# Split weights of w_in kept in DRAM and loaded back, in one inference step of a hybrid backbone

## The chip, the core and the metric

The kernel runs on one core of one Trainium2 chip, as one program that is launched once. The metric is the time on the device in microseconds (us), the median of several runs. The five engines have their own instruction queues, which run in order: PE (TensorE) multiplies matrices, DVE (VectorE) and POOL (GpSimd) do elementwise work, ACT (ScalarE) does activations and copies, and SP (SyncE) issues nearly all transfers between DRAM and the on-chip memory. An instruction that waits on a semaphore holds what stands behind it in its queue.

## The reference

One layer of a backbone is computed for two groups of tokens with the same weights: 256 context tokens and 2,048 latent tokens, each with 1,024 channels, in float32.

```python
h = rms_norm(x, norm1_g) * (1 + sc1) + sh1        # adaLN: sh1, sc1 ... from silu(cond) @ ada_w
z = h @ w_in                                      # 1024 -> 10 column blocks of 256
a_val, a_gate, g_u, g_v, h_q, h_i, h_g, h_ff, h_fb, s5_u = split(z, 10)
o_conv = conformer_conv(a_val, a_gate, ...)       # GLU, depthwise convolution of width 31, LayerNorm, swish
o_gm = chunk_gmlp(g_u, g_v, ...)                  # spatial gating in chunks of 128 positions
o_hg = hgrn_mixer(h_q, h_i, h_g, h_ff, h_fb, ...) # bidirectional gated recurrence, 4 heads of 64
o_s5 = s5_mixer(s5_u, ...)                        # bidirectional diagonal state space, GELU, GLU
x = x + g1 * (concat(o_conv, o_gm, o_hg, o_s5) @ w_out)
x = x + g2 * (relu(h2 @ mlp_w1) ** 2 @ mlp_w2)    # h2: RMSNorm of x, modulated; 1024 -> 4096 -> 1024
y = rms_norm(x, final_norm_g)
```

The scans of the latents start from given states; the final states of the context scans are outputs too.

## The kernel before, in words

**Three products for one.** Large products are made from two parts of each operand: a high part in the type float32r, which is the value rounded by a copy, and a low part, which is the value less its high part. PE adds three products, high by high, low by high and high by low (`gemm_cm`, lines 167 to 176, for channel-major results; `gemm_tm`, lines 558 to 563, for token-major ones). Weights come in units of 128 x 1,024 elements, 0.5 MB each; with a full token block, `gemm_cm` runs 24 matmuls of 512 columns on one unit.

**A unit's way.** `load_unit` (line 162) takes one of three raw tiles `wraw`, has SP load the unit, and calls `split_unit` (line 150). There ACT copies it to a tile `whi` (line 152) and the low part goes to a tile `wlo`, by two halves on POOL (line 157) or by one instruction on DVE (line 159). The argument `pool_only` gives all to POOL (the first pass); otherwise a running count gives every second (second pass) or third unit (third pass) to POOL and the others to DVE. There are four `whi` and four `wlo` tiles, each free again when PE has used it.

**Token blocks and passes.** The tokens are cut into five blocks: the context (256 tokens) and four of 512 latents. The first pass takes blocks 1, 2, 3, 4, 0. For each, `pass1_t` makes values of the recurrence and inputs of the state space, token by token tile, from four units at once; `pass1_g` makes queries and forget gates of two heads at a time, with three units each; `hgrn_local` works inside chunks, in seven levels that pass from PE to DVE, POOL and ACT and back. For the first block `first_block` does most of this with loads of its own, interleaved with the adaLN products, and asks for one unit in `first_out` only. The second pass (`pass2`) takes blocks 0, 1, 2, 3, 4 and asks for ten units for each: four for the convolution's input, two token-major ones at once for the gMLP, two for its other operand, two for the recurrence's output gate. Each block thus loads and splits the units of `w_in` again. Beside the second pass run the state space's scans (`s5_ctx`, `s5_lat`), the first convolutions (`conv`) and the remaining adaLN products (`ada_late`). The third pass (`mix_out`, `mlp_up`, `mlp_down`, `final`) takes `w_out` and the MLP's weights, 368 units of a total of 470.

**What sets the order.** The program is written as generators that are stepped in turn (from line 1297 on). A planner then fixes each engine's order by simulated times and dependencies and places the semaphores; tiles of one tag share a fixed number of buffers, and who writes a buffer next waits until all uses of the tile before it are over. A load thus waits in SP's queue for its buffer, and every transfer behind it in SP's order waits with it.

Of the kernel before, what the change touches and what calls it, by code (L numbers as in the profile page):

```python
# [40 lines left out]
# token blocks: (first token, tokens, conditioning row)  # L41
# [8 lines left out]
# blocks in the order of the first pass; the second starts with the last of them  # L50
# [3 lines left out]
class Carve:  # L54
    """Tiles cut from one, by tag, as from a pool."""
# [19 lines left out]
def trunk_kernel(ctx, tc, I, O):  # L75
# [3 lines left out]
    # ------------------------------------------------------------------ pools  # L79
# [8 lines left out]
    def nm(s):  # L88
        uid[0] += 1
        return f"{s}_{uid[0]}"  # L90
# [19 lines left out]
    # -------------------------------------------------------------- constants  # L110
# [27 lines left out]
    def lower_bounds():  # L138
        """Of the forget gates: cumsum of a softmax over the layers less its first term."""
        V.tensor_tensor(lb, lbl, lbl, ALU.subtract)  # L140
        A.activation(lb, lb, AF.Exp)
        V.reciprocal(lbt, lb)
        V.tensor_tensor(lb, lb, lbt, ALU.mult)
        V.tensor_tensor(lb, lb, lb, ALU.subtract)
        V.tensor_scalar(omlb, lb, -1.0, 1.0, ALU.mult, ALU.add)

    # --------------------------------------------------- weights: load, split
    nlo = [0]

    def split_unit(raw, pool_only, w=1024, every=3):  # L150
        hi = wts.tile([128, 1024], F32R, tag="whi", name=nm("whi"), bufs=4)
        A.activation(hi[:, :w], raw[:, :w], AF.Copy)  # L152
        lo = wts.tile([128, 1024], F32R, tag="wlo", name=nm("wlo"), bufs=4)
# [12 lines left out]

    def gemm_cm(ps, n, unit, hs, ts=None):
        """ps[128 cols, n tokens] = unit[8 k x 128 cols]^T @ hs, of the tokens ts."""
# [9 lines left out]
    # ------------------------------------------------------ adaLN: chunks 0, 1  # L178
# [6 lines left out]
    # ------------------------------------------------------------ DRAM scratch  # L185
# [16 lines left out]
    # ----------------------------------------------------------------- helpers  # L202
    def xblock(pool, b, bufs=1, w=None, halves=1, engs=None, pos=False):
        """x of a block, channel-major, with the position signal on latents."""
# [20 lines left out]
    def rms_rstd(pool, x8, n, eng=None, ps=None, cols=False):  # L225
        """1 / sqrt(mean over channels of x^2 + eps), on every partition."""
# [14 lines left out]
    def rstd_sums(sq, n, ps, heads=1):  # L241
        """Column i * heads + h of ps: sums of sq over a head's channels, for the tokens of tile i."""
# [4 lines left out]
    def rstd_rows(n, scale, ps, heads=1, in_place=False, sums=None):  # L247
        """1 / sqrt(sums * scale + eps), token by token, then spread over the partitions of a head."""
# [30 lines left out]
    def modulate1(pool, hpool, x8, n, rstd, gain, shift, k, w=512, t=None):  # L279
        """hi and lo parts of a channel tile of x * rstd * gain + shift."""  # L280
# [11 lines left out]
    # --------------------------------------------------- S5: tables of a layer  # L292
# [9 lines left out]
    def cmul(eng, o, a, b, tmp):  # L302
        """o = a * b, complex; o may not be a or b."""
# [7 lines left out]
    def s5_small(sp):  # L311
# [10 lines left out]
        # dt = exp(log_dt): Taylor at a 16th of it, then four squarings  # L322
# [8 lines left out]
        # e1 = exp(a_re dt) - 1 by doubling, mag = exp(a_re dt)  # L331
# [42 lines left out]
        # (a_bar - 1) / A  # L374
# [24 lines left out]
        # modulus of a_bar ** 8  # L399
# [3 lines left out]
        # phases e^{i theta n} of the chunk-to-chunk frame, n = 1..16 and n = 0, 16, .., 240  # L403
        V.memset(pc[0][:, :, 0:1], 1.0)
        V.memset(pc[1][:, :, 0:1], 0.0)
        for t_, off, one in ((pb, 0, (u8r.unsqueeze(2), u8i.unsqueeze(2))),
# [3 lines left out]
            m = 1  # L410
# [9 lines left out]
    def s5_tables(sp, scr, small):  # L420
# [12 lines left out]
        # B's for the kernels: a column of 16 each for forward, backward and their sum  # L433
# [3 lines left out]
        # a_bar^m of a quarter's groups, twice over  # L437
# [5 lines left out]
        # the phases of the context, n = 1..32  # L443
# [9 lines left out]
        def cm(o, a, br, bi, g_, n):  # L453
            """o = a * b; o and a [128, (re, im), g_, n], b's parts [128, g_]."""
# [6 lines left out]
        for q in range(4):  # L461
            gs = slice(4 * q, 4 * q + 4)
            # t[:, re or im, 0..3, d] = a_bar^d b_bar and t[:, re or im, 4..7, d] = a_bar^d C^T of the groups
# [12 lines left out]
            # what a chunk's inputs leave in its state, [(dir, p), (s, c)] -> [(s, c), (dir, p)]  # L476
# [10 lines left out]
            # what the state that enters a chunk adds to its outputs  # L487
# [8 lines left out]
            # within a chunk: both directions' kernels, the skip on the diagonal  # L496
# [19 lines left out]
    def s5_kernels():  # L516
        """The kernels within a chunk, spread over its pairs of positions."""
# [4 lines left out]
    # ---------------------------------------------------- adaLN: chunks 2 to 5  # L522
# [14 lines left out]
    # --------------------------------------- first pass: HGRN2 inside of chunks  # L537
# [20 lines left out]
    def gemm_tm(ps, w, xs, wh, wl, first, last):  # L558
        """ps[128 tokens, columns] (+)= x^T @ w, of a channel tile."""
# [32 lines left out]
    def pass1_t(b, hs, p1):  # L592
        """Values of HGRN2 and inputs of S5, token-major."""
        us = [load_unit(I["w_p1t"][i]) for i in range(4)]
# [9 lines left out]
    def pass1_g(b, pair, hs, p1):  # L604
        """Queries and forget gates of two heads; a head's directions share the partitions
        (forward below, backward above), the heads follow each other along the tokens."""
        n = BLOCKS[b][1]
        ps = pg()
        gemm_cm(ps, n, load_unit(I["w_p1c"][3 * pair]), hs)
        qn = q_out(b, ps, p1)  # L610
        f = f_tile(p1)
        for hh in range(2):
            ps = pg()
            gemm_cm(ps, n, load_unit(I["w_p1c"][3 * pair + 1 + hh]), hs)
            f_out(b, 2 * pair + hh, ps, f)
# [8 lines left out]
    def ada_unit(pt, aws, c32, rpool, blocks):  # L624
        """Two blocks of 128 of the adaLN outputs. aws: the weights, four channel tiles each; a tile's
        products go to the partitions of its own, and sel adds them up and turns them."""
# [968 lines left out]
```

## Time and profile before

| what | us |
|---|---|
| median of 3 timed runs | 2892.96 |
| lowest and highest | 2891.01 and 2896.34 |
| span of the profiled execution, first to last instruction | 2886.1 |
| PE busy in that span | 2727.9 (95%) |
| DVE busy | 1975.1 (68%) |
| ACT busy | 1192.9 (41%) |
| POOL busy | 1078.2 (37%) |

The profile is of one execution; its own time is its span, and what the timed runs count beside it lies around the span. The transfers moved 407.43 MB, a mean of 141 GB/s. A busy share is an average over stages with different limits, and matmuls are pipelined, so that PE's busy time is not PE at its peak.

### The profile page before, as it was taken

The numbers are of one execution on the slowest core, as the hardware profiler recorded it, in microseconds if no ns is written. First come the engines' busy times: TensorE is split into PE (matmuls) and PEld (weight loads), VectorE is DVE, ScalarE is ACT, GpSimd is POOL, SyncE is SP. The second block draws the span as 40 slices with busy tenths as digits, with TensorE's granted clock in tenths as the row PEclk, the third lists the DMA queues.
The fourth block names the chain that finished last, engine by engine and source line by source line (L and its number), as shares of the span: only waits on it lengthen the run. The fifth ranks groups of instructions, "written<-read, shape, count | busy, mean of one in ns | idle before, by whom it ended". The sixth has DMA issues, their size and how long they took to land.

```text
span 2886.1 us, 38466 instructions
## 1 busy us (share of the span) xinstructions
PE 2727.9 (95%) x14376; PEld 2260.3 (78%) x14376; DVE 1975.1 (68%) x2786; ACT 1192.9 (41%) x1784; POOL 1078.2 (37%) x915
## 2 busy tenths in 40 slices
PE   6897988899988979999999999999999999999998
PEld 4676878887766769987788888788887888888888
DVE  9889888887799987659973474953384334553336
ACT  4755655553533445443322342332343233433323
POOL 4467757533554534343221232221342111511113
PEclk8999999999999999999999999999999999999999
DMA  8563433357766656634333333333343333233233
GB/s 282 178 187 131 135 118 100 107 167 246 231 188 216 215 197 209 185 124 124 110 102 95 124 123 124 104 101 96 124 149 103 95 98 124 89 131 95 89 101 125
DMA packets 183402, 407.43 MB, mean 141 GB/s; under 512 B 39856, under 2 KB 69680, under 8 KB 182192
## 3 DMA queue, kind: packets, MB, share of 16 engines
q1 hardware_dynamic: 181056, 403.79, 43.4%
q8 instruction: 114, 1.87, 0.3%
q10 hardware_dynamic: 2160, 1.18, 0.1%
q14 instruction: 72, 0.59, 0.1%
HBM read 344.68 MB, written 56.56 MB: 139 GB/s over the span
## 4 chain that ended last, share of the span: by engine, by line
PE 65%; DVE 19%; DMA 2%; issue 2%; POOL 1%; ACT 1%; SPq 0%; DVEq 0%; ACTq 0%; POOLq 0%
PE pg L176 20%; PE pg L175 20%; PE pg L174 20%; DVE x L1166 4%; PE psc L769 2%; DVE wlo L159 1%; DVE m L979 1%; DMA x<-uD 1%; DVE q L775 1%; DVE gg L987 1%; DVE hh L996 1%; DVE pa L271 1%; DVE q L774 1%; DVE kt L773 1%; DVE at L790 1%
## 5 line engine op out<-in xcount | busy, mean ns | idle before, releaser
L174 PE MATMUL pg<-hi,whi 128*128 128x512 f32 (+1 forms) x3488 | 1285.8, 371 | 19.5 <-ACT f L589 5.0
L176 PE MATMUL pg<-hi,wlo 128*128 128x512 f32 (+1 forms) x3488 | 1290.2, 371 | 5.4 <-DVE wlo L159 5.4
L175 PE MATMUL pg<-lo,whi 128*128 128x512 f32 (+1 forms) x3488 | 1288.5, 370 | 3.5 <-DVE lo L286 2.1
L157 POOL TENSOR_TENSOR wlo<-wraw,whi 128x512 fp32r<-128x512 f32 (+1 forms) x404 | 592.1, 1488 | 1281.6 <-ACT whi L152 1198.5
L152 ACT ACTIVATE whi<-wraw 128x1024 fp32r<-128x1024 f32 (+1 forms) x470 | 494.1, 1054 | 873.2 <-PE pg L175 769.9
L174 PEld LDWEIGHTS pg<-hi,whi 128*128 128x128 f32 x3488 | 659.2, 189 | 145.5 <-issue 6.2
L175 PEld LDWEIGHTS pg<-lo,whi 128*128 128x128 f32 x3488 | 659.9, 189 | 129.1 <-issue 7.3
L176 PEld LDWEIGHTS pg<-hi,wlo 128*128 128x128 f32 x3488 | 660.2, 189 | 123.6 <-issue 6.2
L159 DVE TENSOR_TENSOR wlo<-wraw,whi 128x1024 fp32r<-128x1024 f32 x268 | 343.8, 1284 | 198.3 <-ACT whi L152 184.6
L1239 DVE SCALAR_TENSOR_TENSOR x<-pg,adaT,x 128x512 f32<-128x512 f32 (+1 forms) x168 | 111.8, 667 | 283.6 <-PE pg L176 283.1
L1166 DVE SCALAR_TENSOR_TENSOR x<-x,cvw 128x512 f32<-128x512 f32 (+1 forms) x300 | 222.9, 790 | 0.3
L1224 DVE TENSOR_TENSOR t<-t 128x512 f32<-128x512 f32 (+1 forms) x160 | 136.9, 856 | 84.5 <-ACT t L1223 84.5
L1226 ACT ACTIVATE hi<-t 128x512 fp32r<-128x512 f32 (+1 forms) x160 | 94.1, 589 | 240.2 <-DVE t L1224 240.2
L1227 DVE TENSOR_TENSOR lo<-t,hi 128x512 fp32r<-128x512 f32 (+1 forms) x160 | 123.6, 776 | 68.2 <-ACT hi L1226 67.2
L234 POOL TENSOR_TENSOR sq<-sq,sq 128x512 f32<-128x512 f32 (+1 forms) x56 | 87.9, 1570 | 107.8 <-ACT sq L230 107.8
L773 POOL TENSOR_TENSOR kt<-kt,tnx 64x256 f32<-64x256 f32 (+1 forms) x120 | 95.1, 805 | 56.4 <-issue 36.8
L1207 DVE SCALAR_TENSOR_TENSOR x<-pg,adaT,x 128x512 f32<-128x512 f32 (+1 forms) x40 | 27.7, 696 | 112.1 <-PE pg L176 112.1
L230 ACT ACTIVATE sq<-x 128x512 f32<-128x512 f32 (+1 forms) x120 | 66.4, 557 | 81.9 <-DVE sq L234 23.2
L1223 ACT ACTIVATE t<-pg 128x512 f32<-128x512 f32 (+1 forms) x160 | 85.9, 538 | 1.8 <-PE pg L176 1.8
L769 PE MATMUL psc<-qz,kt 128*128 128x128 f32 x432 | 61.0, 299 | 22.8 <-DVE at L790 15.2
L769 PE MATMUL psc<-qzr,kt 128*128 128x128 f32 x576 | 77.1, 286 | 4.3 <-DVE kt L773 3.4
L286 DVE SCALAR_TENSOR_TENSOR lo<-hm,adaT,hi 128x512 fp32r<-128x512 f32 (+1 forms) x72 | 75.8, 1076 | 6.1 <-ACT hi L285 5.2
(372 smaller groups left out, 2982.5 us busy)
## 6 DMA issues: line engine op xcount, KB each, us to landing
wraw<-in_mlp_w_dram SPq DMA_DIRECT2D x328, 512.0 KB, 3.5
wraw<-in_w_p2c_dram SPq DMA_DIRECT2D x40, 512.0 KB, 3.9
wraw<-in_w_out_dram SPq DMA_DIRECT2D x40, 512.0 KB, 3.6
awt<-in_ada_w_dram SPq DMA_DIRECT2D x32, 512.0 KB, 5.6
wraw<-in_w_p1c_dram SPq DMA_DIRECT2D x28, 512.0 KB, 3.6
x<-in_xT_dram SPq DMA_DIRECT2D x16, 512.0 KB, 6.4
aw<-in_ada_w_dram SPq DMA_DIRECT2D x8, 1024.0 KB, 7.3
hD<-hi SPq DMA_DIRECT2D x32, 256.0 KB, 3.3
```

The lines of the kernel that those rows point to most:

```text
L152: A.activation(hi[:, :w], raw[:, :w], AF.Copy)
L157: G.tensor_tensor(lo[:, h_], raw[:, h_], f32(hi[:, h_]), ALU.subtract)
L159: V.tensor_tensor(lo[:, :w], raw[:, :w], f32(hi[:, :w]), ALU.subtract)
L174: PE.matmul(ps[:, :n], wh, xh[:, ts], start=k == 0, stop=False)
L175: PE.matmul(ps[:, :n], wh, xl[:, ts], start=False, stop=False)
L176: PE.matmul(ps[:, :n], wl, xh[:, ts], start=False, stop=k == 7)
L769: PE.matmul(sc[:, s_], kt[:, s_], z[:, s_], start=True, stop=True)
L773: eng.tensor_tensor(kv, kv, tb(lo_, hi_, 1 - half)[:, hs_, :], ALU.mult)
L1166: V.scalar_tensor_tensor(acc[i][:, :n], u2[:, i, k:k + n], cvw[:, i, k:k + 1], acc[i][:, :n], ALU.mult, ALU.add)
L1224: V.tensor_tensor(r, r, r, ALU.mult)
L1227: V.tensor_tensor(lo, r, f32(hi), ALU.subtract)
L1239: V.scalar_tensor_tensor(x8[:, o, ts], ps[:, :n], adaT[:, 40 + o, c:c + 1], x8[:, o, ts], ALU.mult, ALU.add)
```

## The change

The two tiles `whi` and `wlo` of a unit become one tile `whl` that holds both parts, again with four buffers. A new function `kept_unit` takes the place of `load_unit` where weights of `w_in` are asked for. The first time a unit is asked for it is loaded and split as before, and both parts, 1 MB, are stored to a DRAM tile of its own. Each later time both parts are loaded from there by one transfer into the `whl` tile; no raw tile is used and nothing is split. The running count then does not move. `first_block` keeps its own loads, and the weights of `w_out` and the MLP go through `load_unit` as before. The diff also drops comments, which are left out here.

```diff
-    def split_unit(raw, pool_only, w=1024, every=3):
-        hi = wts.tile([128, 1024], F32R, tag="whi", name=nm("whi"), bufs=4)
+    def wtile():
+        return wts.tile([128, 2, 1024], F32R, tag="whl", name=nm("whl"), bufs=4)
+
+    def split_unit(raw, pool_only, w=1024, every=3, t=None):
+        t = t or wtile()
+        hi, lo = t[:, 0, :], t[:, 1, :]
         A.activation(hi[:, :w], raw[:, :w], AF.Copy)
-        lo = wts.tile([128, 1024], F32R, tag="wlo", name=nm("wlo"), bufs=4)
         nlo[0] += 1
...
+    kept = {}
+
+    def kept_unit(name, i, pool_only=True, every=3, keep=True):
+        t = wtile()
+        if (name, i) in kept:
+            SP.dma_start(f32(t), f32(kept[name, i]))
+            return t[:, 0, :], t[:, 1, :]
+        raw = wts.tile([128, 1024], F32, tag="wraw", name=nm("wraw"), bufs=3)
+        SP.dma_start(raw, I[name][i])
+        split_unit(raw, pool_only, every=every, t=t)
+        kept[name, i] = dt_(f"{name}_hl{i}", [128, 2, 1024], F32R)
+        SP.dma_start(f32(kept[name, i]), f32(t))
+        return t[:, 0, :], t[:, 1, :]
...
-        us = [load_unit(I["w_p1t"][i]) for i in range(4)]
+        us = [kept_unit("w_p1t", i) for i in range(4)]
...
-        gemm_cm(ps, n, load_unit(I["w_p1c"][3 * pair]), hs)
+        gemm_cm(ps, n, kept_unit("w_p1c", 3 * pair), hs)
...
-            gemm_cm(ps, n, load_unit(I["w_p1c"][3 * pair + 1 + hh]), hs)
+            gemm_cm(ps, n, kept_unit("w_p1c", 3 * pair + 1 + hh), hs)
...
-        gemm_cm(ps, n, load_unit(I["w_p1c"][2]), hs)
+        gemm_cm(ps, n, kept_unit("w_p1c", 2), hs)
...
-            gemm_cm(pgate, n, load_unit(I["w_p2c"][2 + i], False, 2), hs)
+            gemm_cm(pgate, n, kept_unit("w_p2c", 2 + i, False, 2), hs)
...
-            gemm_cm(pv, n, load_unit(I["w_p2c"][i], False, 2), hs)
+            gemm_cm(pv, n, kept_unit("w_p2c", i, False, 2), hs)
...
-        us = [load_unit(I["w_p2t"][i], False, 2) for i in range(2)]
+        us = [kept_unit("w_p2t", i, False, 2) for i in range(2)]
...
-            gemm_cm(pu, n, load_unit(I["w_p2c"][4 + pair], False, 2), hs)
+            gemm_cm(pu, n, kept_unit("w_p2c", 4 + pair, False, 2), hs)
...
-            gemm_cm(pz, n, load_unit(I["w_p2c"][6 + pair], False, 2), hs)
+            gemm_cm(pz, n, kept_unit("w_p2c", 6 + pair, False, 2), hs)
```

## Rows read from the trace of the kernel before

**Rows 1.** The profile's page, part 2: busy tenths in 40 slices of the span.
```profile
PE   6897988899988979999999999999999999999998
DVE  9889888887799987659973474953384334553336
```

**Rows 2.** Windows: length, busy us of PE, PEld, DVE, ACT, POOL; clock, DMA, GB/s.
```profile
170.00:490.00 320.00, 284.44 (x1665) 244.44 (x1664) 279.57 (x375) 184.30 (x284) 220.01 (x203) 0.95 0.38 122
570.00:930.00 360.00, 325.39 (x2045) 262.84 (x2044) 316.78 (x550) 151.01 (x275) 170.03 (x191) 0.95 0.65 213
650.00:700.00 50.00, 48.59 (x254) 38.99 (x253) 40.66 (x79) 13.98 (x22) 10.28 (x10) 0.90 0.86 301
850.00:900.00 50.00, 43.50 (x239) 32.32 (x232) 49.68 (x76) 18.38 (x27) 23.71 (x25) 0.90 0.73 245
1450.00:1500.00 50.00, 49.80 (x216) 40.04 (x215) 44.45 (x55) 12.28 (x14) 12.45 (x7) 1.00 0.33 106
```

**Rows 3.** Chain of waits by line, 250:600 us, then 720:1060 us.
```profile
by line: PE psc L769 13.8%; PE pg L174 8.5%; PE pg L175 8.2%; PE pg L176 8.2%; DVE q L775 6.3%; DVE q L774 4.8%; DVE kt L773 4.7%; issue 4.6%; DVE at L790 4.5%; PE psc L811 3.0%; DVE Sl L838 3.0%; POOL x L222 2.9%; PE psc L737 2.1%; PE psc 
by line: DVE x L1166 11.2%; DVE m L979 9.7%; issue 6.5%; DVE gg L987 5.8%; DVE hh L996 5.7%; DVE wlo L159 4.8%; DVE pa L271 4.6%; DVE hh L995 4.4%; PE pg L174 4.4%; PE pg L175 4.3%; PE pg L176 4.1%; PE pg L1080 1.7%; DMA x<-mixD 1.7%; PE pg
```

**Rows 4.** Windows of L157 alone: length, POOL's busy us (instructions).
```profile
170.00:490.00 320.00, 94.74 (x63) 0.95 0.38 122
300.00:350.00 50.00, 28.59 (x18) 1.00 0.37 112
350.00:400.00 50.00, 2.52 (x2) 0.93 0.45 156
570.00:930.00 360.00, 55.58 (x40) 0.95 0.65 213
```

**Rows 5.** Window of L159 alone: length, DVE's busy us (instructions).
```profile
570.00:930.00 360.00, 27.27 (x20) 0.95 0.65 213
```

**Rows 6.** The page, part 5: line L152 in the whole run.
```profile
L152 ACT ACTIVATE whi<-wraw 128x1024 fp32r<-128x1024 f32 (+1 forms) x470 | 494.1, 1054 | 873.2 <-PE pg L175 769.9
```

**Rows 7.** Groups by form, DVE, 170:490 us: busy us, mean ns.
```profile
L775 DVE TENSOR_TENSOR q<-q,tnx 64x512 f32<-64x512 f32 x38 | 41.7, 1100 | 1.1
L773 DVE TENSOR_TENSOR kt<-kt,tnx 64x256 f32<-64x256 f32 x70 | 41.3, 605 | 12.1 <-PE psc L769 11.8
L774 DVE TENSOR_TENSOR q<-q,tnx 64x512 f32<-64x512 f32 x38 | 37.4, 987 | 3.1 <-ACT qz L762 2.0 <-DVE tnx L782 0.5
```

**Rows 8.** Single lines: L775 in 300:350, then L775 and L773 in 350:400.
```profile
L775 DVE TENSOR_TENSOR q<-q,tnx x6: 691/1666/1679, 303.7 to 345.1; 64x512 f32<-64x512 f32 x6
L775 DVE TENSOR_TENSOR q<-q,tnx x6: 687/689/690, 362.7 to 398.1; 64x512 f32<-64x512 f32 x6
L773 DVE TENSOR_TENSOR kt<-kt,tnx x14: 397/413/970, 352.4 to 399.9; 64x256 f32<-64x256 f32 x14
```

**Rows 9.** Groups by form, DVE, 570:930 us.
```profile
L1166 DVE SCALAR_TENSOR_TENSOR x<-x,cvw 128x512 f32<-128x512 f32 x58 | 50.5, 893 | 0.3
```

**Rows 10.** Single line: L1166 in 1350:1500 us.
```profile
L1166 DVE SCALAR_TENSOR_TENSOR x<-x,cvw x97: 732/740/1790, 1350.2 to 1486.5; 128x512 f32<-128x512 f32 x97
```

**Rows 11.** Waits of SP's DMA queue, 0:1100 us: total us, times, longest us.
```profile
SPq L164 <- POOL wlo L157: 136.0, 52, 5.8
SPq L164 <- DVE wlo L159: 81.3, 19, 9.8
```

**Rows 12.** Waits of ACT, 600:1060 us.
```profile
ACT whi L152 <- PE pg L175: 45.7, 15, 17.8
```

**Rows 13.** DMA issues of the whole run: KB each, median us to landing.
```profile
wraw<-in_w_p1t_dram SPq DMA_DIRECT2D x16, 512.0 KB, 3.5
wraw<-in_w_p2t_dram SPq DMA_DIRECT2D x10, 512.0 KB, 5.3
x<-in_xT_dram SPq DMA_DIRECT2D x1, 1024.0 KB, 5.1
aw<-in_ada_w_dram SPq DMA_DIRECT2D x8, 1024.0 KB, 7.3
```

## The prediction

> **What bounds the kernel now.** I read the picture of forty slices first. TensorE (PE) shows nearly full slices from about 1,150 us to the end; ahead of that its digits move between 6 and 9, and there VectorE (DVE) carries the 8s and 9s [rows 1]. So only the first 1,150 us have time to give back, and the changed lines lie inside them. The two stretches where weights of `w_in` would be reloaded are 170:490 us (rest of the first pass) and 570:930 us (second pass behind its first block). In the first PE is busy 284 of 320 us and DVE 280; in the second 325 and 317 of 360 [rows 2]. Looked at closer, from 850 to 900 us DVE is full (49.7 of 50) while PE is not (43.5) [rows 2].
>
> PE's busy time also flatters it, since matmuls overlap. A saturated stretch, 1450:1500 us, fits 216 matmuls of 512 columns, one per 0.23 us, so a unit of 24 takes 5.6 us; in 850:900 us, where none has more columns and many have fewer, only 239 stand in the same 50 us [rows 2]. The page "Perfetto Trace Analysis" of the Trainium skill (Identifying the Most-Contended Engine) says to judge TensorE by weight loads, not by matmul busy time; by it PE in 850:900 us, at 32.3 us of loads against 40.0 in the saturated stretch, would have about a fifth of its time to spare, not the 6.5 us of the busy column. This trace agrees.
>
> The chain of waits says the same: in 720:1060 us it runs mainly through DVE lines, L159, the low parts of weights, among them with 4.8% of 340 us, 16 us. In 250:600 us it alternates between PE (L769 and the products) and DVE (L773 to L775, L790) [rows 3]. The first pass is a ping-pong of two engines; the second is bound by DVE.
>
> **The change, part by part.** Counting calls: the first pass asks for 44 units (16 token-major and 28 column ones), the second for 50. Of these 94, 20 are first uses, which are split as before and then stored; 74 become reloads: 34 in the first pass, 40 in the second. A reload is one transfer of 1 MB instead of 0.5 MB, with no ACT copy, no subtraction and no raw tile.
>
> *Removed from ACT and POOL.* The 74 copies at 1.05 us are 78 us of ACT [rows 6]. The stretch 170:490 us holds 63 POOL halves (94.7 of POOL's 220 us); 570:930 us holds 40 halves (55.6 of 170 us) and 20 low parts on DVE (27.3 us) [rows 2, 4, 5]. Nearly all of these belong to reloads after the change. Neither ACT nor POOL is full, so their 78 and 150 us are not a gain by themselves; they matter through what they hold up.
>
> *First pass: DVE's stalls beside POOL.* DVE's operations get long when POOL runs splits. L775 takes 1,666 ns (median) in 300:350 us and 689 ns in 350:400 us [rows 8]; the first of these holds 18 halves, the second 2, while POOL's other work goes on [rows 4]. Against the medians of 350:400 us, the means over 170:490 us cost L775 38 x (1,100 - 689) = 15.6 us, L774, of the same shape, 38 x (987 - 689) = 11.3 us and L773 70 x (605 - 413) = 13.4 us, 40 us together [rows 7, 8]. Shared by POOL's time the splits own 94.7 / 220 of it, 17 us; at the other end all 40. The 300:350 row is the nearest, so I take 28 us. "SBUF — State Buffer" of the Trainium skill (Who interferes with whom) calls this an exclusive lock that the later instruction waits out whole; by that, each of the 63 halves could cost up to its own 1.5 us, 95 us in all. The rows hold no more than the 40 us in these lines, so the sum stays with them. What reaches the end: DVE is busy 87% of this stretch, but PE is nearly as full, and the splits run just where the products run on PE. I pass on a bit under half: **13 us** (ends 0 and 40).
>
> *Second pass: direct DVE work and stalls.* The 20 low parts, 27.3 us, leave the engine that bounds [rows 5]. To this come stalls beside 40 fewer POOL halves: the convolution alone is 58 x (893 - 740) = 9 us longer than its median in 1350:1500 us [rows 9, 10]. POOL's splits are a third of POOL's time there, but other DVE lines gain too; I take 8 us (ends 3 and 15). Of 35 us some falls where DVE is not full, before 750 us: passing three quarters on gives **26 us** (ends 10 and 42).
>
> *Blocked queues.* ACT's copy waits for PE to free a weight buffer, 45.7 us in 15 waits between 600 and 1060 us, one of them 17.8 us [rows 12]; behind it in ACT's queue stand the S5 scan's evacuations, which DVE and PE want. With a reload that wait moves to SP. Ends 0 and 20; most of these waits lie under a busy DVE, so **5 us**.
>
> *Added: later weights.* Today three raw tiles are fetched ahead of the four split buffers. A reload writes into a split buffer itself, so it starts only when PE is done with the unit four before it, and its wait stands at the head of SP's queue; behind it wait the loads of h, the stores of results and the S5 tables, and PE, DVE and ACT behind those. In a run of column units three buffers hold 3 x 5.6 = 16.7 us of products, and a 1 MB load lands in 5.1 us (the one of x) to 7.3 us (adaLN's weights, on busy queues) [rows 2, 13], so it is hidden. It is not where all buffers empty together: the first-pass step that uses four units at once (three times with reloads), and more weakly the two-unit gMLP step of the second pass (four times). There the next unit was split in about 1.05 + 1.5 us (a copy and a POOL half) from a raw tile already there and now needs 5.1 to 7.3 us: 2.6 to 4.8 us more, at 3 to 7 places: **8 us** lost (ends 0 and 34).
>
> *Added: traffic.* 39 MB more loads and 21 MB of stores on SP's queue. In 570:930 us 40 x 0.52 MB add 58 GB/s to 213, and the share of the DMA engines goes from 0.65 to about 0.83; 650:700 us shows that 0.86 at 301 GB/s can be had [rows 2]. The stores follow the first splits, ten ahead of 170 us and ten between the two stretches; PE holds the buffer for products meanwhile anyway. I cost them at nothing; if a store holds SP or a buffer, up to 20 x 1 us. The third pass is untouched, except that the one-in-three turn of POOL and DVE shifts by one unit (74 fewer counts), worth nothing either way.
>
> Sum: 13 + 26 + 5 - 8 = 36 us. The profiled span is 2,886.1 us, so 2,850 after; the median of the timed runs lies 6.9 us above that span (2,892.96), which I keep: **2,857 us**.
>
> **The rivals.** *More of it comes through.* If the ping-pong of the first pass is really DVE's, and blocked queues cost what they show, the relief is 40 + 35 + 20 us with no loss: 2,893 - 95 = 2,798 us at the far end, 2,815 as a middle. For: DVE's 87 to 99% busy columns; against: PE is as full in the first pass.
>
> *It goes nowhere.* Both stretches could be bound by the round trips between PE, ACT and DVE, so that shorter DVE work only lengthens its waits: gain under 6 us, 2,890 us. For: the chain in 250:600 us is mixed [rows 3]; against: 20 instructions leave a stretch that is 99% busy.
>
> *Slower: SP runs dry of buffers.* A reload waits for PE and holds all of SP's queue, with three raw tiles of lead gone. SP already waits 136 us for POOL's and 81 us for DVE's low parts ahead of weight loads, up to 9.8 us at a time [rows 11]. If at the seven places where buffers empty together the next unit comes 10 us late (such a wait, rather than a landing alone), that is 70 us against 44 us of gain: 2,893 + 26 = 2,919 us. It decides from 44 / 7 = 6.3 us a place. For: loads in busy stretches land later, 5.3 us at the median for the units of the gMLP step against 3.5 us for the same size in the first pass [rows 13]. "DMA: Bandwidth & Descriptors" of the Trainium skill (Latency and other measured facts) has memory latency grow tenfold under high load, to 2 us; the two medians point that way, by half and not tenfold. Against: four buffers still hold three times a landing.
>
> **How the numbers follow.** Forecast (gain of 12 to 60 us) 0.48, more comes through 0.18, goes nowhere 0.13, slower 0.21. A measurement of this kernel can tell 0.2%, about 6 us, from no change: faster 0.66, same 0.13, slower 0.21. The likeliest case alone spans 2,833 to 2,881 us; to leave out no more than 2 in 10, the range takes most of both outer cases: 2,805 to 2,912 us.
>
> **What would show it.** Right: 74 fewer ACT copies (396 left), 108 fewer POOL halves and 20 fewer DVE low parts; L775 near 690 to 800 ns on average in the first pass; DVE less full from 600 to 900 us and the steady stretch beginning some 36 us earlier; everything behind it as long as before. Wrong: PE waiting on transfers of reloaded weights for several us at a time behind the four-unit steps, SP's waits on PE longer than all its waits on splits now, or unchanged DVE means beside a POOL that is free of splits.

## The result and the profile after

The changed kernel takes 2871.49 us (median of 4 runs, 2869.65 to 2875.35), the kernel before on the same chip 2891.99 us (4 runs, 2890.69 to 2896.34). The ratio is 0.9928, with a 95% interval of 0.9913 to 0.9942: 20.5 us faster, where 36 had been forecast. The direction and the range held; the size was little more than half. The profiled execution after has a span of 2867.9 us, 18.2 us less than before.

The first and second parts of the page of the changed kernel (busy us and number of instructions of each engine; busy tenths in 40 slices):

```profile
PE 2711.8 (95%) x14376; PEld 2247.5 (78%) x14376; DVE 1887.3 (66%) x2766; ACT 1109.4 (39%) x1710; POOL 915.7 (32%) x807
PE   6798999899999869999999999999999999999998
DVE  8879677966799986669873474943474334553336
```

DVE lost 88 us of work, ACT 84 and POOL 163, and the time fell by 20. Against [rows 1] DVE's first two slices are an 8 each where they were a 9 and an 8, and PE's second is a 7 and not an 8: the beginning became emptier, and nothing was removed there.

Parts 5 and 6 of the same page: the three lines that split weights, then the reloads (KB each, median us from issue to landing):

```profile
L160 POOL TENSOR_TENSOR whl<-wraw,whl 128x512 fp32r<-128x512 f32 (+1 forms) x296 | 434.2, 1488 | 1199.7 <-ACT whl L156 1133.4
L156 ACT ACTIVATE whl<-wraw 128x1024 fp32r<-128x1024 f32 (+1 forms) x396 | 415.5, 1052 | 600.6 <-PE pg L194 459.0
L162 DVE TENSOR_TENSOR whl<-wraw,whl 128x1024 fp32r<-128x1024 f32 x248 | 309.5, 1249 | 65.2 <-ACT whl L156 63.7
...
whl<-w_p2c_hl SPq DMA_DIRECT2D x32, 1024.0 KB, 7.5
whl<-w_p1c_hl SPq DMA_DIRECT2D x22, 1024.0 KB, 7.6
whl<-w_p1t_hl SPq DMA_DIRECT2D x12, 1024.0 KB, 5.0
```

The counts are the ones predicted: 396 copies (470 before, [rows 6]), 296 halves and 248 low parts. The reloads land in 5.0 to 7.6 us, about the range that [rows 13] had given (5.1 to 7.3 us for 1 MB).

Windows of the changed kernel, and last a window of the kernel before that was not shown ahead of the prediction (columns as in [rows 2]):

```profile
100.00:200.00 100.00, 83.06 (x370) 65.76 (x370) 73.14 (x87) 60.10 (x95) 44.18 (x35) 0.91 0.88 300
170.00:490.00 320.00, 289.50 (x1734) 249.48 (x1735) 255.20 (x393) 161.05 (x264) 129.13 (x153) 0.96 0.55 188
570.00:930.00 360.00, 338.13 (x2172) 273.29 (x2171) 288.44 (x543) 117.95 (x247) 124.48 (x156) 0.98 0.82 284
850.00:900.00 50.00, 43.90 (x248) 32.29 (x247) 49.51 (x77) 11.85 (x20) 20.56 (x23) 0.94 0.84 300
```

```profile
100.00:200.00 100.00, 89.38 (x413) 70.07 (x412) 80.14 (x86) 65.58 (x101) 58.43 (x45) 0.97 0.61 192
```

Against [rows 2] DVE's busy time falls by 24 us in the rest of the first pass and by 28 us in the second, and PE does more products in both (1,734 for 1,665 and 2,172 for 2,045). But 850 to 900 us is as before, DVE full and PE at 44 of 50. And from 100 to 200 us, where eight of the twenty stores are issued (two lie just ahead, at 79 and 87 us), PE does 43 products fewer and the DMA engines are busy 88% of the time instead of 61%.

Two lines mark how far the kernel has come: the last masked copy of the recurrence ends the first pass's work (L790 before, L808 after), and the last scan of the latents' state space (L987, L1005) lies in the second pass. In these rows of single lines, before and then after, the two times behind the durations are the first and the last start:

```profile
L790 DVE COPY_PREDICATED at<-masks,psc x50: 706/1328/1370, 184.6 to 634.9; 128x1024 f32<-128x1024 int32 x40, 128x512 f32<-128x512 int32 x10
L987 DVE TENSOR_TENSOR_SCAN gg<-rt,s,m x32: 653/739/1717, 760.2 to 1049.6; 128x256 f32<-128x256 f32 x32
```

```profile
L808 DVE COPY_PREDICATED at<-masks,psc x50: 709/1328/1354, 192.6 to 615.6; 128x1024 f32<-128x1024 int32 x40, 128x512 f32<-128x512 int32 x10
L1005 DVE TENSOR_TENSOR_SCAN gg<-rt,s,m x32: 645/742/1769, 746.1 to 1026.4; 128x256 f32<-128x256 f32 x32
```

The changed kernel starts the masked copies 8 us late, ends them 19 us early, and ends the scans 23 us early. These two lines are read in each experiment below.

### The profile page after: what moved, and what is told of

Its sections match the earlier page's. It is cut to its first block, busy times and chain, and to the rows that moved or that the text cites. A ratio compares the mean times of both kernels' runs of the same rounds, so it can differ in the third digit from the quotient of the medians.

```text
span 2867.9 us, 38038 instructions
## 1 busy us (share of the span) xinstructions
PE 2711.8 (95%) x14376; PEld 2247.5 (78%) x14376; DVE 1887.3 (66%) x2766; ACT 1109.4 (39%) x1710; POOL 915.7 (32%) x807
## 4 chain that ended last, share of the span: by engine, by line
PE 59%; DVE 12%; DMA 3%; issue 1%; ACT 0%; POOL 0%; SPq 0%; DVEq 0%; ACTq 0%
PE pg L194 19%; PE pg L193 19%; PE pg L192 19%; DVE x L1184 3%; DVE m L997 1%; DVE whl L162 1%; DVE gg L1005 1%; DVE hh L1014 1%; DVE pa L289 1%; DMA x<-uD 1%; DMA whl<-w_p2c_hl 1%; DVE hh L1013 0%; DMA x<-in_xT_dram 0%; DVE lo L304 0%; PE pb L1051 0%
## 5 line engine op out<-in xcount | busy, mean ns | idle before, releaser
L194 PE MATMUL pg<-hi,whl 128*128 128x512 f32 (+1 forms) x3488 | 1287.5, 370 | 8.3 <-DVE whl L162 8.2
L192 PE MATMUL pg<-hi,whl 128*128 128x512 f32 (+1 forms) x3488 | 1284.8, 371 | 10.0 <-ACT whl L156 3.5
L193 PE MATMUL pg<-lo,whl 128*128 128x512 f32 (+1 forms) x3488 | 1287.2, 370 | 4.6 <-DVE lo L1245 3.0
L160 POOL TENSOR_TENSOR whl<-wraw,whl 128x512 fp32r<-128x512 f32 (+1 forms) x296 | 434.2, 1488 | 1199.7 <-ACT whl L156 1133.4
L192 PEld LDWEIGHTS pg<-hi,whl 128*128 128x128 f32 x3488 | 658.2, 189 | 133.0 <-issue 6.6
L193 PEld LDWEIGHTS pg<-lo,whl 128*128 128x128 f32 x3488 | 659.2, 189 | 129.3 <-issue 7.4
L194 PEld LDWEIGHTS pg<-hi,whl 128*128 128x128 f32 x3488 | 659.3, 189 | 127.3 <-DVE whl L162 8.9
L156 ACT ACTIVATE whl<-wraw 128x1024 fp32r<-128x1024 f32 (+1 forms) x396 | 415.5, 1052 | 600.6 <-PE pg L194 459.0
L162 DVE TENSOR_TENSOR whl<-wraw,whl 128x1024 fp32r<-128x1024 f32 x248 | 309.5, 1249 | 65.2 <-ACT whl L156 63.7
L1242 DVE TENSOR_TENSOR t<-t 128x512 f32<-128x512 f32 (+1 forms) x160 | 115.7, 724 | 252.4 <-ACT t L1241 252.0
L787 PEld LDWEIGHTS psc<-qzr,kt 128*128 128x128 f32 x576 | 72.6, 201 | 14.5 <-POOL kt L791 7.9
L303 ACT ACTIVATE hi<-hm,adaT 128x512 fp32r<-128x512 f32 (+1 forms) x72 | 49.5, 697 | 67.3 <-DVE hm L301 63.3
```

The lines of the kernel that those rows point to most:

```text
L160: G.tensor_tensor(lo[:, h_], raw[:, h_], f32(hi[:, h_]), ALU.subtract)
L162: V.tensor_tensor(lo[:, :w], raw[:, :w], f32(hi[:, :w]), ALU.subtract)
L192: PE.matmul(ps[:, :n], wh, xh[:, ts], start=k == 0, stop=False)
L193: PE.matmul(ps[:, :n], wh, xl[:, ts], start=False, stop=False)
L194: PE.matmul(ps[:, :n], wl, xh[:, ts], start=False, stop=k == 7)
L787: PE.matmul(sc[:, s_], kt[:, s_], z[:, s_], start=True, stop=True)
```

## The experiments

Each kernel ran beside the kernel before on its chip, in five rounds. The table gathers the readings: the median, its ratio to the kernel before with the 95% interval, and, of the profiled execution, the first and last masked copy and the last scan, in us.

| kernel | median | ratio (interval) | first copy | last copy | last scan |
|---|---|---|---|---|---|
| before | 2891.99 | 1 | 184.6 | 634.9 | 1049.6 |
| after | 2871.49 | 0.9928 (0.9913 to 0.9942) | 192.6 | 615.6 | 1026.4 |
| e1, reloads in the first pass only | 2893.41 | 1.0011 (1.0003 to 1.0019) | 194.2 | 624.7 | 1055.0 |
| e2, reloads in the second pass only | 2879.88 | 0.9959 (0.9946 to 0.9972) | 188.7 | 637.8 | 1038.9 |
| e3, half the reload | 2869.51 | 0.9923 (0.9911 to 0.9935) | 192.1 | 620.0 | 1029.3 |
| e4, each store twice | 2901.72 | 1.0036 (1.0024 to 1.0047) | 217.0 | 630.0 | 1054.1 |
| e5, the joint tile alone | 2913.16 | 1.0069 (1.0049 to 1.009) | 191.3 | 649.2 | 1075.6 |
| e6, two tiles again, reloads and stores in halves | 2867.53 | 0.9911 (0.9892 to 0.993) | 200.5 | 614.6 | 1016.4 |
| e7, before without first-pass low parts | 2885.56 | 0.9981 (0.9969 to 0.9994) | 183.0 | 612.5 | 1043.2 |
| e8, before without DVE's second-pass low parts | 2889.74 | 0.9992 (0.998 to 1.0004) | 186.6 | 630.9 | 1051.0 |
| e9, before without any reused low part | 2852.98 | 0.987 (0.9857 to 0.9884) | 182.7 | 609.2 | 1013.2 |
| e10, before with equal instructions swapped | 2892.26 | 1.0006 (0.9996 to 1.0016) | 187.1 | 635.5 | 1051.3 |
| e11, e6 with the stores on ACT's queue | 2873.49 | 0.9946 (0.9932 to 0.996) | 197.4 | 614.6 | 1032.8 |
| e12, only ACT's copies removed | 2929.01 | 1.0133 (1.0119 to 1.0146) | 190.5 | 649.1 | 1076.1 |

### One pass at a time

In e1 the second pass goes back to `load_unit`, in e2 the first; the joint tile stays in both.

```diff
-            gemm_cm(pgate, n, kept_unit("w_p2c", 2 + i, False, 2), hs)
+            gemm_cm(pgate, n, load_unit(I["w_p2c"][2 + i], False, 2), hs)
...
```

> Reloads in the first pass only; the second pass loads and splits as before. Theory A (the first pass's relief of DVE makes its recurrence end about 20 us earlier, DVE carries that lead into the second pass and cashes it where DVE binds): 8 to 12 us faster than the kernel before, about 2,882 us. Theory B (in the first pass PE is full where the splits run, so the relief is lost; all of the gain is the second pass's own): within 3 us of the kernel before, about 2,891 us.

> Reloads in the second pass only; the first pass loads and splits as before. Theory A: 8 to 12 us faster than the kernel before, about 2,882 us. Theory B: 17 to 21 us faster, about 2,872 us, as the whole change.

Reloads in the first pass alone gain nothing (3 us lost), those in the second pass alone 10 us. 10 less 3 is 7, and both together give 20: against the kernel before the two don't add up, and neither theory had that. A price that is counted twice can cover this: e1, e2 and the changed kernel all have the joint tile, which by itself costs 20 us (e5, below; whether it costs as much beside reloads is not shown). Against e5, at 1.0069, the first pass's reloads are worth 17 us, the second's 32 and both together 41, less than their sum.

Against the kernel before, e1 is 10 us ahead at the last masked copy and 5 us behind at the last scan. That alone does not show that the first pass's lead was given back, since the second pass of e1 splits into the joint tile, as e5's does. The same two lines in e5, then in e1:

```profile
L808 DVE COPY_PREDICATED at<-masks,psc x50: 708/1322/1374, 191.3 to 649.2; 128x1024 f32<-128x1024 int32 x40, 128x512 f32<-128x512 int32 x10
L1005 DVE TENSOR_TENSOR_SCAN gg<-rt,s,m x32: 649/741/1762, 784.7 to 1075.6; 128x256 f32<-128x256 f32 x32
```

```profile
L808 DVE COPY_PREDICATED at<-masks,psc x50: 708/1327/1362, 194.2 to 624.7; 128x1024 f32<-128x1024 int32 x40, 128x512 f32<-128x512 int32 x10
L1005 DVE TENSOR_TENSOR_SCAN gg<-rt,s,m x32: 719/744/1706, 761.3 to 1055.0; 128x256 f32<-128x256 f32 x32
```

Against e5, e1 leads by 25 us at the last masked copy and by 21 at the last scan: there most of the lead is kept.

### What the transfers cost

In e3 a reload brings the high part only, which then serves as both; in e4 each of the twenty units is stored a second time, to a place that nobody reads.

```diff
-            SP.dma_start(f32(t), f32(kept[name, i]))
-            return t[:, 0, :], t[:, 1, :]
+            SP.dma_start(f32(t[:, 0, :]), f32(kept[name, i][:, 0, :]))
+            return t[:, 0, :], t[:, 0, :]
```

```diff
         SP.dma_start(f32(kept[name, i]), f32(t))
+        SP.dma_start(f32(dt_(f"{name}_hx{i}", [128, 2, 1024], F32R)), f32(t))
```

> As the changed kernel, but a reload brings the high part alone (0.5 MB), and PE uses it in the place of the low part too: the low parts of reloaded weights are left out, the number of matmuls is the same. Theory C (1 MB reloads land late and cost 8 us or more): at least 8 us faster than the changed kernel, 2,863 us or less. Theory D (the reloads are hidden): within 3 us of it, about 2,871 us.

> As the changed kernel, but each of the 20 split units is stored twice, to two scratch tiles. The recurrence's first step ended 4 us later in the changed kernel than before. If the stores did that (SP waits for the split, 1 MB each): another 4 us or more, 2,876 us or above. If the stores are hidden: within 3 us of the changed kernel.

Half the bytes change the time by 2 us, inside the intervals: the size of the reloads is hidden. Twenty more stores cost 30 us. The window of e4 in which eight of the first ten lie:

```profile
100.00:200.00 100.00, 69.96 (x292) 53.95 (x292) 60.98 (x74) 45.86 (x75) 38.09 (x31) 0.87 0.95 353
```

PE's products fall from 370 to 292 there, with the DMA engines at 95%, and the first masked copy starts at 217.0 us, 24 us behind the changed kernel. Doubling is no measure of the first store; but it shows that stores in these two places are not free.

### The joint tile

In e5 every unit is loaded and split as before, into the joint tile. In e6 the change keeps its reloads, but `whi` and `wlo` are two tiles again, and reload and store are two transfers of 0.5 MB each.

```diff
-        return wts.tile([128, 2, 1024], F32R, tag="whl", name=nm("whl"), bufs=4)
+        return [wts.tile([128, 1024], F32R, tag=tag, name=nm(tag), bufs=4) for tag in ("whi", "wlo")]
...
-            SP.dma_start(f32(t), f32(kept[name, i]))
+            for j in range(2):
+                SP.dma_start(f32(t[j]), f32(kept[name, i][:, j, :]))
```

> The changed kernel's joint tile for both parts, and nothing else of the change: all units of w_in are loaded and split each time. With reloads in one pass only, PE's work was 9 to 12 us behind the kernel before in whichever pass still split. Theory E (the joint tile, or the order planned for it, costs that in each pass where units are split): 8 to 20 us slower than the kernel before, 2,898 to 2,910 us. Theory F (the tile is neutral and the lag came from the reloads next to it): within 3 us, about 2,890 us.

> The change with separate tiles for the high and low parts, as before it: a part is stored and reloaded by a transfer of its own, 0.5 MB each. Theory E: faster than the changed kernel by 5 to 15 us, 2,857 to 2,866 us. Theory F: within 3 us of it or, for twice the transfers on SP's queue, up to 5 us slower, 2,870 to 2,876 us.

The joint tile by itself makes the kernel before 0.69% (interval 0.49 to 0.9%) slower, 20 us. Beside the reloads, e6 with separate tiles is at 0.9911 and the changed kernel at 0.9928; the intervals overlap, so that whatever the joint tile costs there is not told from nothing. e6 is the fastest version that leaves nothing of the computation out.

Of e5's loss 7 us are there at the first masked copy, 14 at the last, and at the last scan all of it (26 us; its span is 27 us longer). The first part stands where the changed kernel has its stores, and e5 stores nothing. The window of e5, then of e6:

```profile
100.00:200.00 100.00, 80.69 (x360) 63.94 (x359) 82.16 (x94) 63.52 (x102) 58.55 (x45) 0.90 0.61 192
```

```profile
100.00:200.00 100.00, 86.11 (x364) 68.79 (x363) 61.87 (x75) 54.63 (x87) 41.06 (x33) 0.89 0.90 300
```

The joint tile without stores takes PE from 413 products to 360, with the DMA engines as busy as before (61%), and separate tiles with the stores take it to 364; the changed kernel, which has both, has 370. So the products that the changed kernel lacks there can't be put down to its stores alone.

The end of e5's loss shows in 1100:1150 us. Windows, and PE's waits (us in total, times, longest) of e5:

```profile
1100.00:1150.00 50.00, 39.87 (x282) 34.66 (x281) 35.67 (x42) 22.78 (x33) 23.47 (x16) 0.86 0.68 237
```

```profile
PE pb L1051 <- DVE yo L1046: 9.4, 2, 5.6
```

In the kernel before the same window is already steady:

```profile
1100.00:1150.00 50.00, 49.24 (x419) 49.04 (x418) 35.16 (x47) 29.38 (x44) 17.15 (x13) 1.00 0.72 231
```

In e5 PE stands before a product that DVE's S5 output feeds: the work behind the second pass has slid. A mere other order by the planner was the next suspect, and e10 tried it: the kernel before, with three pairs of equal, independent instructions swapped in the program (one pair shown).

```diff
-            A.activation(v4(z, 0, 64, 1), v4(q, 0, 64, 1), AF.Copy)
             A.activation(v4(z, 64, 128, 0), v4(q, 64, 128, 0), AF.Copy)
+            A.activation(v4(z, 0, 64, 1), v4(q, 0, 64, 1), AF.Copy)
...
```

> The kernel before, with three pairs of independent instructions of equal size in the recurrence's levels written in the other order: the work is the same, only the planner's order can move. If the planned order by itself moves the time as far as the joint tile did: more than 5 us from the kernel before, either way. If not: within 3 us, and the 20 us of the joint tile are the tile's own.

It moves the time by 1 us, within its interval. One such shuffle is a small sample, but it gives no support to scatter of 20 us. Why the joint tile alone costs that stays open.

### What the relief is worth without the reloads

Here the kernel before keeps its loads, copies, raw tiles and separate tiles, and the low parts of reused units are left out (the high part is used twice): in e7 those of the first pass, 68 POOL halves; in e8 the 20 that DVE makes in the second pass; in e9 all of both passes, so also 40 POOL halves of the second.

```diff
+    def again(name, i, pool_only=True, every=3):
+        if (name, i) not in seen:
+            seen.add((name, i))
+            return load_unit(I[name][i], pool_only, every)
+        raw = wts.tile([128, 1024], F32, tag="wraw", name=nm("wraw"), bufs=3)
+        SP.dma_start(raw, I[name][i])
+        hi = wts.tile([128, 1024], F32R, tag="whi", name=nm("whi"), bufs=4)
+        A.activation(hi, raw, AF.Copy)
+        nlo[0] += 1
+        return hi, hi
```

> The kernel before, with the low parts of the 34 units that the first pass asks for again left out (PE uses the high part twice): 68 POOL halves fewer, loads, copies, tiles and matmuls as before. Theory A (the relief of DVE in the first pass is worth something by itself): 8 us faster or more, 2,882 us or less. Theory B (PE is full where the splits run): within 3 us of the kernel before.

> The kernel before, with the 20 low parts that DVE makes for units the second pass asks for again left out: 27 us of DVE, nothing of POOL, ACT, loads or tiles. If DVE's direct work is the second pass's gain: 12 to 22 us faster, 2,868 to 2,878 us. If the gain there is from POOL's stalls or from ACT's queue: 6 us faster or less, 2,884 us or more.

> The kernel before, with the low parts of all 74 units that are asked for again left out (PE uses the high part twice): 108 POOL halves and 20 DVE instructions fewer; loads, copies, tiles and matmuls as before. The parts alone gave 5 us (first pass) and 1 us (DVE's of the second). If the low parts are what the reloads win by: about 2,868 us, as with reloads into two tiles. If ACT's copies, with their waits for PE at the head of ACT's queue, are the larger share: 2,880 us or more.

e7 wins 5 us (interval 0.9969 to 0.9994), between the bounds of its two theories; e8 2 us, not told from nothing; e9 38 us, 15 more than expected. The rows of single lines say how, e7 first and then e9:

```profile
L805 DVE COPY_PREDICATED at<-masks,psc x50: 707/1332/1376, 183.0 to 612.5; 128x1024 f32<-128x1024 int32 x40, 128x512 f32<-128x512 int32 x10
L1002 DVE TENSOR_TENSOR_SCAN gg<-rt,s,m x32: 718/742/1275, 747.6 to 1043.2; 128x256 f32<-128x256 f32 x32
```

```profile
L803 DVE COPY_PREDICATED at<-masks,psc x50: 707/1329/1372, 182.7 to 609.2; 128x1024 f32<-128x1024 int32 x40, 128x512 f32<-128x512 int32 x10
L1000 DVE TENSOR_TENSOR_SCAN gg<-rt,s,m x32: 719/742/1224, 737.4 to 1013.2; 128x256 f32<-128x256 f32 x32
```

e7 reaches the last masked copy 22 us early and the last scan only 6 us early. e9 is hardly further at the first (26 us) but holds and adds to it: 36 us at the last scan. So the first pass's relief is real, and in e7 most of it is lost in a second pass that stays as it was. With the joint tile (e5 to e1) 17 us of 25 reached the end: how much is lost depends on the kernel around it.

e8 shows that DVE's 20 low parts alone don't relieve the second pass. Its window, the first of DVE's waits in the same stretch, and the same three waits before:

```profile
570.00:930.00 360.00, 330.56 (x2068) 266.27 (x2069) 295.27 (x535) 152.40 (x280) 172.16 (x193) 0.95 0.65 213
```

```profile
DVE hh L1007 <- DMA s5yDc<-yc: 10.8, 1, 10.8
DVE m L994 <- ACT d L988: 8.0, 3, 4.2
DVE x L1178 <- POOL x L1167: 6.4, 1, 6.4
```

```profile
DVE hh L992 <- DMA s5yDc<-yc: 6.0, 1, 6.0
DVE m L979 <- ACT d L973: 2.6, 1, 2.6
DVE x L1163 <- POOL x L1152: 3.4, 1, 3.4
```

DVE's busy time falls by 21.5 us against [rows 2], PE's products rise only from 2,045 to 2,068, and DVE waits instead. Summed over all its waits there, it stands 16.2 us for POOL where it was 5.6, 24.5 for ACT (15.5) and 13.5 for transfers (6.0), and less for PE, 6.4 (12.1). What e9 has beyond e7 and e8 is the 40 POOL halves of the second pass and the relief of both passes at once; those halves alone were not run, so which of the two carries the gain stays open.

Two other things could help e9. A raw tile is free there once ACT has copied it, but SP stood as long ahead of loads of weights as before, 312 us against 315 in 0:1100 us. ACT's copies, all kept, wait less for PE in 600:1060 us, 23 us in three rows against 50 in two; this is the largest row, against the 45.7 of [rows 12]:

```profile
ACT whi L176 <- PE pg L189: 18.3, 8, 4.5
```

So e9's 38 us may hold some relief of ACT's queue too.

### The copies and the queues

e12 removes only ACT's copies: the high part is reloaded, the raw unit is loaded too, and the low part is made each time. e11 takes e6 and issues its stores from ACT's queue.

```diff
+            raw = wts.tile([128, 1024], F32, tag="wraw", name=nm("wraw"), bufs=3)
+            SP.dma_start(raw, I[name][i])
+            SP.dma_start(f32(t[0]), f32(kept[name, i]))
+            return split_unit(raw, pool_only, every=every, t=t, copy=False)
```

```diff
-            SP.dma_start(f32(kept[name, i][:, j, :]), f32(t[j]))
+            A.dma_start(f32(kept[name, i][:, j, :]), f32(t[j]))
```

> Two tiles as before; of a unit asked for again the high part is reloaded (0.5 MB) and the raw unit is loaded too (0.5 MB), and the low part is made from both as before: only the 74 ACT copies go. If ACT's copies are the larger share: 8 us faster than the kernel before or more, 2,882 us or less. If the low parts are: within 3 us, or slower by the added transfers, 2,888 us or more.

> Two tiles with reloads, and the 40 half-unit stores are issued from ACT's queue instead of SP's. If SP, waiting for a split at the head of its queue, is what stores cost: 4 us or more faster than with SP's stores, 2,863 us or less. If the wait only moves to ACT: 2,867 us or more.

e12 loses 38 us: without 74 copies, ACT is busy 71 us less (1,122.0 of 1,192.9) and the kernel is slower. Two of the longest waits of SP's queue in 0:1100 us of e12:

```profile
SPq L178 <- POOL wlo L161: 104.6, 33, 6.8
SPq L179 <- PE pg L197: 55.2, 24, 7.3
```

Raw loads (L178) still wait for the splits, as in [rows 11], and behind them in the same queue the high parts (L179) now wait for PE. So e12 gives no price for the copies alone. e11 is 6 us slower than e6 by the medians and 10 by the ratios (0.9946 against 0.9911, the intervals just apart): moving the stores to ACT's queue gains nothing.

## Why the prediction was right in sign and too large

**What bounds the kernel.** Right: the steady stretch is untouched, and all that was won lies ahead of 1,050 us.

**First pass, 13 us.** The size was fair, and the way to it was not. POOL's splits did hold DVE; the groups by form of DVE after, 170:490 us (busy us, mean ns | idle before them and its releaser), and one of them in e7, where POOL's halves alone are left out:

```profile
L791 DVE TENSOR_TENSOR kt<-kt,tnx 64x256 f32<-64x256 f32 x74 | 36.5, 508 | 19.1 <-PE psc L787 18.7
L793 DVE TENSOR_TENSOR q<-q,tnx 64x512 f32<-64x512 f32 x39 | 32.2, 825 | 1.2
L792 DVE TENSOR_TENSOR q<-q,tnx 64x512 f32<-64x512 f32 x39 | 31.8, 815 | 0.4
```

```profile
L790 DVE TENSOR_TENSOR q<-q,tnx 64x512 f32<-64x512 f32 x41 | 33.2, 813 | 2.1 <-ACT qz L778 0.9
```

Against [rows 7] the means fall from 1,100 to 825 ns, from 987 to 815 and from 605 to 508; 690 to 800 was forecast for the first, so that some 25 us of the 40 left and not 28, which were a choice between 17 and 40 (39 x 275 + 39 x 172 + 74 x 97 ns). This agrees in direction with "SBUF — State Buffer" of the Trainium skill (Who interferes with whom), which has such a clash wait for the other instruction whole; the 95 us that the prediction worked out by it were not seen. The line that feeds on PE waits more than it did. DVE's waits on PE there, 170:640 us, before and after:

```profile
DVE kt L773 <- PE psc L769: 23.0, 20, 5.2
```

```profile
DVE kt L791 <- PE psc L787: 46.6, 20, 10.1
```

They grew by 23.6 us: much of what DVE no longer works it now waits for PE, the ping-pong that the prediction described. Priced at the end of the kernel the first pass's relief is 5 us with separate tiles and the second pass as it was (e7), and 9 to 17 us between kernels with the joint tile: 0.9928 against 0.9959 (after and e2) and 1.0011 against 1.0069 (e1 and e5).

**Second pass, 26 us.** The size again held, roughly; the carrier did not, as far as it was tested. On two bases the whole relief of the second pass is worth 32 us: from e7 to e9, 0.9981 to 0.987, and from e5 to e2, 1.0069 to 0.9959, the second with its ten stores paid. But the step "the 20 low parts, 27.3 us, leave the engine that bounds" failed: done alone it is worth 2 us (e8); what it is worth beside a freer POOL no run shows. An engine at 88% of a stretch [rows 2] is not the only one in it; the time taken from it came back as waits for POOL, ACT and transfers. The convolution beside a freer POOL did get shorter; its group by form after, 570:930 us:

```profile
L1184 DVE SCALAR_TENSOR_TENSOR x<-x,cvw 128x512 f32<-128x512 f32 x60 | 48.9, 827 | 0.5
```

893 ns in [rows 9] became 827, 4 us in 60 instructions, half of the 9 that the rows had offered.

**Blocked ACT queue, 5 us.** Neither shown nor ruled out. ACT's 45.7 us of waits [rows 12] are gone for reloads; e9 keeps every copy and is the fastest kernel, but its copies wait half as long; e12 removes the copies and loses, with reloads added to SP's queue.

**The gains together** were 13 + 26 + 5 = 44 us; e9, which has the first two without the costs and perhaps part of the third, gives 38 (2,890.93 - 2,852.98).

**The step that failed** is the price on the other side: "I cost them at nothing; if a store holds SP or a buffer, up to 20 x 1 us", and with it later weights at 8 us; what the joint tile adds was never costed at all. What reloads, stores and the joint tile cost is the distance from e9: 17 us for the changed kernel (38.0 - 20.5), and 15 by the medians (38.0 - 22.9) or 12 by the ratios for e6, which has no joint tile. Against 44 us of gains and 8 of loss in the forecast the runs thus give 38 and 17: of the miss of 15.5 us some 6 lie in the gains and 9 to 10 in the price. Where the price lies: the size of the reloads costs nothing (e3), and PE stood before reloaded weights in 170:930 us for less than 1 us; these are all its waits on them:

```profile
PE pg L192 <- DMA whl<-w_p1c_hl: 0.7, 1, 0.7
```

Two parts are left. Stores: doubling them costs 30 us, 1.5 us for each, over the prediction's bound, and in the changed kernel SP stood 52 us in 0:1100 us with a store at the head of its queue (all rows of L182 together, the largest below). That the first set costs as much as the second is not shown, since no kernel with reloads and without stores ran. The joint tile: 20 us by itself (e5), not told from nothing beside the reloads (e6). The 8 us that are gone by the first masked copy don't decide between them: e5, which stores nothing, is 7 us late there, and e6, with the stores and two tiles, 16. How the 17 us divide stays open.

**The slower rival** had the right mechanism and too high a price. SP's queue after, 0:1100 us:

```profile
SPq L176 <- PE pg L194: 100.2, 27, 10.8
SPq L167 <- DVE whl L162: 26.2, 11, 8.2
SPq L182 <- POOL whl L160: 20.4, 8, 6.6
SPq L176 <- PE pg L581: 14.8, 10, 4.2
```

Reloads (L176) wait 100 us for one line of PE at the head of the queue, up to 10.8 us at a time, and 144 us for all lines of PE together; this is under the 217 us that loads waited for splits [rows 11]. No wait of PE on a reload comes near the 6.3 us a place from which that rival decides. "It goes nowhere" (under 6 us) holds for e8 and, just, for e7, each a part of the change; "more comes through" did not happen anywhere, since even e9 gains less than the 60 us where that case began.

## What to carry to other kernels

Relief of a busy engine in one stage is only a lead: follow it through the next stage, where it can be given back, and price two reliefs together before adding them up. Work taken from an engine that is nearly full is worth its time only if nothing else in that stretch is as late, so its waits by source are to be read beside its busy share. A part of a change that has a price of its own (here the joint tile) belongs into the base as well when other parts are tried one by one; otherwise its price is counted in each of them. What a cache of results costs to fill (stores where the queues are fullest, and the buffers these hold) is priced like the work it saves.

## What was not expected of the hardware

The clock granted to PE differs between these kernels although they do the same products. Span and mean granted clock of e5 and e9, then of the kernel before:

```profile
core 0: 2913.1 us, clock 0.966
```

```profile
core 0: 2853.1 us, clock 0.981
```

```profile
core 0: 2886.1 us, clock 0.975
```

The means mix two levels, 2.4 and 1.2 GHz; behind 1,150 us the mean is 1.00 in every kernel whose window was read, so all the difference lies ahead. Other runs of the kernel before lie between 0.970 and 0.980. Time weighted by what is missing to full clock is 99 us in e5 (2913.1 x 0.034), 72 us before and 54 us in e9: differences of 27 and 18 us, as large as much of what was measured. Stretches with gaps on PE often have the low values (0.86 in 1100:1150 us of e5, PE busy 39.9 of 50; 1.00 before, 49.2 of 50), but not always: 650:700 us before has 0.90 with PE busy 48.6 of 50 [rows 2]. It isn't the whole story: e2 has 0.972, lower than before, and is 10 us faster. Whether the lower clock lengthens the gaps or only follows them, no run here tells apart.
